# Seven products in place of eight for three pairs of cross-attention query blocks and five pairs of gate blocks

## The chip, the cores and the metric

The kernel runs on one core of one Trainium2 chip. The metric is the device time of one execution in microseconds (us). TensorE is called PE here, VectorE DVE or Vector, ScalarE ACT or Scalar, GpSimd POOL, and SyncE SP.

## The reference

Two transformer blocks are applied one after the other to one sequence of 512 tokens with 1024 features, all in float32. The two projections that the change touches are the queries of block 1's cross-attention to a memory of 256 rows, and the two kinds of gates of block 2:

```python
# block 1
x = x + hybrid_mixer(rmsnorm(x, norm_mix), ...)
h = rmsnorm(x, norm_xa)
q = (h @ w_q).reshape(b, s, 4, 256)          # xa_wq, 1024 x 1024
scores = einsum('bshd,bmhd->bhsm', q, k) * 256 ** -0.5
x = x + (softmax(scores) @ v) @ w_o          # xa_wo
x = x + squared_relu_mlp(rmsnorm(x, norm_ffn), w1, w2)
x = rmsnorm(x, norm_final)
# block 2
u = rmsnorm_2(x, norm_mix_w)
cb, cc, cx, q, k, v, g_conv, g_attn = split(u @ w_in + b_in)   # w_in_2
y_conv = (cb * causal_dwconv(cc * cx)) @ w_conv_out
y_attn = sliding_window_attention(rope(q), rope(k), v) @ w_attn_out + b_attn_out
merged = sigmoid(g_conv) * y_conv + sigmoid(g_attn) * y_attn
x = x + merged @ w_mix_out
... a gated feed-forward network with a causal convolution, and a last norm
```

Each of `g_conv` and `g_attn` is 1024 columns wide.

## The kernel before, in words

**Layout.** Everything is kept transposed: features lie on the 128 partitions, the 512 tokens along the free dimension. A projection to 128 output columns (a block, numbered n) over 1024 inputs is eight weight tiles of 128 x 128.

**Products.** PE works in the type f32r. For accuracy every operand is split into a high part, rounded to f32r, and a low part, the rest; `mm3` (L482 to L484) multiplies one weight tile with one operand in three matmuls (high by high, high by low, low by high). A plain block is 24 matmuls of 512 columns.

**Weights.** They stream from DRAM in the order in which `weight_order` lists them, eight tiles (1024 columns) in a unit. `prefetch` loads a unit into one of `NRAW` raw buffers, Scalar writes the high part (L279) and Vector the low part (L281) into one of `NWS` pairs of buffers `whi` and `wlo`. A weight index counts the tiles used. `defer(n, f)` emits f when the index has advanced by n, and `flush` does so for what is due. The order of issue on SP is that of the program. The other engines' orders are made by a list scheduler, which takes the program's order as priority and lets ready work go ahead.

**Seven products.** Twenty-six pairs of blocks (in the two feed-forward networks) are computed in the Strassen-Winograd manner. `pairg` takes two blocks and two halves of the tokens as a 2 x 2 problem, and makes seven products instead of eight, each over four pairs p of input blocks: 84 matmuls of 256 columns for two blocks. The products are ordered 1, 5, 2, 7, 3, 6, 4 (`SEVEN`, L364). `seven_steps` makes the weight sums of a pair from two raw units and splits them (L318, L326, L331, L336, L339). `rights` makes the operands on the other side: for each p, two scaled copies on Scalar (L426, L427), five operations of 256 columns on Vector (L432 to L437), and two splits (L550, L551), which leave V and W of that p in four buffers that last. Products 1, 2 and 3 use only the plain split activations; products 5 and 7 need V, 6 and 4 need W. The two results of a pair are put together in a tile `q`: after product 5 a copy of the first bank (L401), then, after the products, L407, L408, L409 and L410, which read the other three banks. The second of the two results comes out negated.

**Buffers.** `NSLOT` buffers of 2 KB (tag `t2`) hold all other tiles of 512 columns, `NQ` the tiles `q`. Eight PSUM banks are split into four `mm` and four `sm`; `bank(kind)` hands out the four of a kind in turn.

**Cross-attention.** After `w_out`, `q_g` computes the eight query blocks, n from 0 to 7, and splits them. Each of four heads needs two of them. `drive` runs the heads, which are chains of short dependent steps, and fills PE in between with `q_g` and then `wo_g` (the first part of the output projection `xa_wo`).

**Block 2's gates.** `gated_g` computes gate 30, then `w_conv_out_2` (eight blocks), then the gates 31 to 37, each a plain block, multiplied with `rb` (the row norm), put through a sigmoid and multiplied into `yc`. Between them it emits `norm_x(n)` (L1442), which scales x for the residual. After the attention, a loop computes the gates 38 to 45, each followed by a block of `w_attn_out_2` (four tiles), and splits the merged result for `w_mix_out_2`.

Of the kernel before, what the change touches and what calls it, by code (L numbers as in the profile page):

```python
# [18 lines left out]
T = 512  # L19
D = 1024  # L20

NSLOT = 67
NRAW, NWS = 4, 5

NSR, NQ = 2, 2


SPREAD = [6, 2]
# [31 lines left out]
def weight_order():  # L60


    seq = []
    seven = set()

    def pair(name, n1, n2):
        assert len(seq) % 8 == 0
        seven.add(len(seq) // 8)
        for n, o in ((n1, 0), (n2, 1), (n1, 1), (n2, 0)):
            for k in range(o, 8, 2):  # L70
                seq.append((name, k, n))

    def cols(name, ns, ks):
        for n in ns:
            for k in ks:
                seq.append((name, k, n))

    def rows(name, ks, ns):
        for k in ks:
            for n in ns:  # L80
                seq.append((name, k, n))

    r8 = range(8)
    for lo in (12, 8, 16):
        cols("w_in", range(lo, lo + 4), r8)
    rows("w_in", r8, range(4, 8))
    cols("w_in", range(0, 4), r8)
    cols("w_in", range(20, 24), r8)
    cols("xa_wk", r8, r8)
    rows("xa_wv", r8, range(4))  # L90
    rows("xa_wv", r8, range(4, 8))
    cols("w_out", range(NWO), range(4))
    cols("w_out", range(NWO), range(4, 8))
    cols("w_out", range(NWO, 8), r8)
    cols("xa_wq", r8, r8)
    cols("xa_wo", range(4), range(6))
    cols("xa_wo", range(4), (6, 7))
    cols("xa_wo", range(4, 8), r8)
    for what, i, g in ffn_order():
        if what == 1 and i < NPLAIN:  # L100
            cols("ffn_w1", (2 * i, 2 * i + 1), r8)
        elif what == 1:
            pair("ffn_w1", 2 * i, 2 * i + 1)
        else:
            cols("ffn_w2", [i], range(8 * g, 8 * g + 8))

    cols("w_in_2", [28, 29, 24, 25, 26, 27], r8)
    for i in range(8):
        cols("w_in_2", [8 + i, 16 + i, i], r8)
    cols("w_in_2", [30], r8)  # L110
    cols("w_conv_out_2", r8, r8)
    cols("w_in_2", range(31, 38), r8)
    for i in range(8):
        cols("w_in_2", [38 + i], r8)
        cols("w_attn_out_2", [i], range(4))
    cols("w_mix_out_2", r8, r8)
    for what, i, g in ffn2_order():
        if what == 2:
            cols("w_ffn_down_2", [i], range(*GROUPS2[g]))
        elif i in SEVEN2:  # L120
            pair("w_ffn_up_2", i, 22 + i)
        else:
            cols("w_ffn_up_2", [i, 22 + i], r8)
    cols("w_ffn_down_2", r8, range(*GROUPS2[2]))
    return seq, seven
# [64 lines left out]
def _build(ctx, tc, nc, A, out, stage):  # L190
# [18 lines left out]
    def tmp(shape=(P, T)):  # L209
        return ap_.tile(list(shape), F32, tag="t2", bufs=NSLOT, name=nm("tmp"))  # L210

# [29 lines left out]
    def col(name, i=0, n=1):  # L241
        o = COFF[name][0] + i
        return colt[:, o:o + n]
# [166 lines left out]
        V.tensor_tensor(q4[:, 1:3, :], b3(3), q4[:, 1:3, :], op=ALU.add)  # L410
        then(q)

    def rights(x, gname, xs):


        H = T // 2
        f = lambda hl, j: (hl[0][:, j * H:(j + 1) * H], hl[1][:, j * H:(j + 1) * H])
        res = [{} for _ in range(len(xs) // 2)]
        steps = []

        def one(p):
            st = {}

            def s0():
                st["a"], st["b"] = t2(), t2()
                S.activation(st["a"], x[2 * p], AF.Copy, scale=col(gname, 2 * p))  # L426
                S.activation(st["b"], x[2 * p + 1], AF.Copy, scale=col(gname, 2 * p + 1))  # L427

            def s1():
                a, b = st["a"], st["b"]  # L430
                st["v"], st["w"] = v, w = t2(), t2()
                V.tensor_sub(v[:, H:], b[:, H:], a[:, H:])  # L432
                V.scalar_tensor_tensor(out=w[:, :H], in0=a[:, H:], scalar=1.0, in1=a[:, :H],
                                       op0=ALU.mult, op1=ALU.subtract)
                V.tensor_scalar_mul(v[:, :H], w[:, :H], -1.0)
                V.tensor_sub(w[:, :H], w[:, :H], b[:, H:])
                V.scalar_tensor_tensor(out=w[:, H:], in0=w[:, :H], scalar=-1.0, in1=b[:, :H],  # L437
                                       op0=ALU.mult, op1=ALU.subtract)

            def s2():  # L440
                vs = split(st["v"])
                ws = split(st["w"])
                res[p].update({"B11": f(xs[2 * p], 0), "B21": f(xs[2 * p + 1], 0), "B22": f(xs[2 * p + 1], 1),
                               "V1": f(vs, 0), "V7": f(vs, 1), "V6": f(ws, 0), "T4": f(ws, 1)})

            return [s0, s1, s2]

        for p in range(len(xs) // 2):
            steps.extend(one(p))
        return res, steps  # L450
# [793 lines left out]
    os_ = []  # L1244
    qq = []

    def q_g():
        for n in range(8):
            ps = bank()
            yield from ling("xa_wq", n, range(8), xs, ps)  # L1250
            qq.append(split(ps))

    def head(h):
        while len(qq) < 2 * h + 2:
# [72 lines left out]

    rb2 = acc_tile()
    wide_later(acc, 1e-6, rb2, WIDE1, True)
    rops, steps = rights(x, "norm_ffn", xs)  # L1330
    for j, f in enumerate(steps):
        defer(1 + VD * (j // 3) + j % 3, f)
    cosT, sinT = acc_tile(), acc_tile()
# [123 lines left out]
        V.tensor_mul(t, ps, rb)  # L1457
        return t

    def biased(n):  # L1460
        g = proj_g(n)
        while True:
            try:
                next(g)
            except StopIteration as e:
                return e.value

    def rope(n, t, then):

# [166 lines left out]
            cs_.append((hi, lo))  # L1636

    yc = []

    def gated_g():  # L1640
        sg0 = None
        for n in range(-1, 8):
            if n == -1:
                t = yield from proj_g(30)
                sg0 = t2()
                S.activation(sg0, t, AF.Sigmoid, bias=col("b_in_2", 30))
                continue
            ps = bank()
            yield from ling("w_conv_out_2", n, range(8), cs_, ps)
            y = t2()  # L1650
            if n == 0:
                V.tensor_mul(y, ps, sg0)
            else:
                S.copy(y, ps)
            yc.append(y)
        for i in range(1, 8):
            norm_x(i - 1)
            t = yield from proj_g(30 + i)
            S.activation(t, t, AF.Sigmoid, bias=col("b_in_2", 30 + i))
            V.tensor_mul(yc[i], yc[i], t)  # L1660
        norm_x(7)

    bg.append(kvq_g())
    bg.append(conv2_g())
# [3 lines left out]
    flush()  # L1668
    ms = []
    for i in range(8):  # L1670
        t = biased(38 + i)
        g = tmp()
        S.activation(g, t, AF.Sigmoid, bias=col("b_in_2", 38 + i))
        ps = lin("w_attn_out_2", i, range(4), at)
        V.scalar_tensor_tensor(out=g, in0=ps, scalar=col("b_attn_out_2", i), in1=g, op0=ALU.add, op1=ALU.mult)
        V.tensor_add(yc[i], yc[i], g)
        ms.append(split(yc[i]))
# [12 lines left out]
    rb = acc_tile()  # L1690
    wide_later(acc, 1e-5, rb, 8, False)

    rops2, steps = rights(x, "norm_ffn_w_2", xs)
    for j, f in enumerate(steps):
        defer(8 + 10 * (j // 3) + 2 * (j % 3), f)

# [227 lines left out]
```

## Time and profile before

| | |
|---|---|
| median of three runs | 1541.34 us (1540.96 to 1542.74) |
| the profiled execution | 1543.6 us, of which the span of the trace is 1541.8 |
| mean granted clock of PE | 0.995 |
| PE busy | 1507.0 us of the span |
| Vector busy | 1074.0 us |
| Scalar busy | 707.1 us |
| matmuls | 8336 |

Busy times are sums over an engine's instructions. Matmuls follow each other in a pipeline, so their cost in a dense stretch is read from the distance between starts, not from their listed durations.

### The profile page before, as it was taken

How to read it: one execution, taken by the hardware profiler on the slowest of the kernel's cores; microseconds unless marked ns; L12 is line 12 of the kernel's file. 1: busy time of each engine (PE TensorE's matmuls, PEld its weight loads, DVE VectorE, ACT ScalarE, POOL GpSimd, SP SyncE). 2: the span in 40 equal slices, each digit the busy share in tenths (PEclk: the TensorE clock that was granted, in tenths of full speed). 3: DMA queues.
4: the chain of work that ended last, by engine and by line, in shares of the span. 5: the costliest groups of instructions: out<-in, count | busy, mean ns of one | idle time of the engine just before them, and what ended most of it. 6: DMA issues, size and time to landing. Idle time of an engine off the chain costs nothing.

```text
span 1541.8 us, 21393 instructions
## 1 busy us (share of the span) xinstructions
PE 1507.0 (98%) x8336; PEld 1290.3 (84%) x8336; DVE 1074.0 (70%) x1759; ACT 707.1 (46%) x1169; POOL 150.8 (10%) x162
## 2 busy tenths in 40 slices
PE   8999999999999999999999999999999998999996
PEld 6888898888888888989888888888888887898986
DVE  6897675554786786767688767335547887779757
ACT  5665555443564353535444434333334443344333
POOL 0002120200201202011400000000020001101201
PEclk9999999999999999999999999999999999999998
DMA  6033335221223223324044222222222222323311
GB/s 254 17 114 94 116 125 204 95 69 55 82 69 110 96 90 109 109 83 137 14 143 138 82 82 83 72 94 94 96 96 82 82 82 96 98 80 110 125 54 55
DMA packets 51509, 149.94 MB, mean 97 GB/s; under 512 B 9552, under 2 KB 14032, under 8 KB 51408
## 3 DMA queue, kind: packets, MB, share of 16 engines
q1 hardware_dynamic: 51264, 148.32, 28.5%
q8 instruction: 65, 1.06, 0.3%
q14 instruction: 36, 0.29, 0.1%
q10 hardware_dynamic: 144, 0.26, 0.1%
HBM read 143.97 MB, written 3.28 MB: 96 GB/s over the span
## 4 chain that ended last, share of the span: by engine, by line
PE 92%; DVE 4%; ACT 2%; issue 1%; DMA 1%; POOL 0%; SPq 0%; DVEq 0%; ACTq 0%; POOLq 0%
PE mm L482 26%; PE mm L483 25%; PE mm L484 25%; PE sm L484 3%; PE sm L482 3%; PE sm L483 3%; ACT whi L279 1%; DMA raw<-wts 1%; DVE wlo L281 0%; ACT t L1111 0%; PE sm L602 0%; DVE t L1825 0%; PE sm L920 0%; PE sm L1597 0%; PE sm L1596 0%
## 5 line engine op out<-in xcount | busy, mean ns | idle before, releaser
L482 PE MATMUL mm<-t,whi 128*128 128x512 f32 (+1 forms) x1840 | 686.0, 373 | 9.3 <-ACT whi L275 7.1
L483 PE MATMUL mm<-t,whi 128*128 128x512 f32 (+1 forms) x1840 | 682.9, 371 | 0.2 <-DVE t L551 0.2
L484 PE MATMUL mm<-t,wlo 128*128 128x512 f32 (+1 forms) x1840 | 682.5, 371 | 0.0
L482 PEld LDWEIGHTS mm<-t,whi 128*128 128x128 f32 x1840 | 347.4, 189 | 70.3 <-ACT whi L275 7.1
L484 PEld LDWEIGHTS mm<-t,wlo 128*128 128x128 f32 x1840 | 347.2, 189 | 63.3 <-DVE wlo L281 0.5
L483 PEld LDWEIGHTS mm<-t,whi 128*128 128x128 f32 x1840 | 347.4, 189 | 61.2 <-DVE t L551 0.7
L279 ACT CAST whi<-raw 128x1024 fp32r<-128x1024 f32 x202 | 211.2, 1051 | 303.6 <-PE mm L483 142.8
L281 DVE TENSOR_TENSOR wlo<-raw,whi 128x1024 fp32r<-128x1024 f32 x184 | 228.6, 1243 | 75.8 <-ACT whi L279 75.4
L596 POOL TENSOR_TENSOR acc<-acc,tmp 128x512 f32<-128x512 f32 (+1 forms) x37 | 52.7, 1430 | 467.7 <-ACT tmp L592 467.4
L482 PE MATMUL sm<-t,whi 128*128 128x256 f32 (+1 forms) x320 | 90.9, 284 | 2.9 <-ACT whi L326 2.9
L483 PE MATMUL sm<-t,whi 128*128 128x256 f32 (+1 forms) x320 | 90.8, 284 | 1.6 <-DVE t L551 1.6
L484 PE MATMUL sm<-t,wlo 128*128 128x256 f32 (+1 forms) x320 | 90.9, 284 | 0.8 <-DVE wlo L331 0.8
L331 DVE TENSOR_TENSOR wlo<-sraw,whi 128x1024 fp32r<-128x1024 f32 x52 | 68.8, 1325 | 30.9 <-ACT whi L326 30.6
L326 ACT CAST whi<-sraw 128x1024 fp32r<-128x1024 f32 x52 | 54.6, 1049 | 70.5 <-PE mm L483 59.9
L1457 DVE TENSOR_TENSOR tmp<-mm,acc 128x512 f32<-128x512 f32 x46 | 31.7, 690 | 49.0 <-PE mm L484 46.9
L482 PEld LDWEIGHTS sm<-t,whi 128*128 128x128 f32 x320 | 60.2, 188 | 4.0 <-ACT whi L326 3.3
L1414 POOL TENSOR_TENSOR res<-res,tmp 128x512 f32<-128x512 f32 x24 | 39.0, 1637 | 248.4 <-DVE tmp L1412 236.8
L483 PEld LDWEIGHTS sm<-t,whi 128*128 128x128 f32 x320 | 60.2, 188 | 2.5 <-DVE t L551 1.8
L484 PEld LDWEIGHTS sm<-t,wlo 128*128 128x128 f32 x320 | 60.4, 189 | 1.5 <-DVE wlo L331 1.0
L326 ACT CAST whi<-raw 128x1024 fp32r<-128x1024 f32 x26 | 27.3, 1050 | 51.7 <-PE mm L483 24.9
L318 DVE TENSOR_TENSOR sraw<-raw,raw 128x1024 f32<-128x1024 f32 x26 | 34.4, 1325 | 21.6 <-DMA raw<-wts 21.6
L1744 POOL TENSOR_TENSOR res<-res,tmp 128x512 f32<-128x512 f32 x16 | 27.6, 1734 | 164.9 <-DVE tmp L1743 164.9
(384 smaller groups left out, 1998.1 us busy)
## 6 DMA issues: line engine op xcount, KB each, us to landing
raw<-wts SPq DMA_DIRECT2D x259, 512.0 KB, 3.3
res<-xT SPq DMA_DIRECT2D x16, 256.0 KB, 5.2
yT<-t SPq DMA_DIRECT2D x6, 256.0 KB, 2.2
tmp<-tmp SPq DMA_DIRECT2D x20, 64.0 KB, 2.0
gm<-gm SPq DMA_DIRECT2D x4, 256.0 KB, 4.6
dn<-ch SPq DMA_DIRECT2D x4, 256.0 KB, 2.3
tmp<-memT SPq DMA_DIRECT2D x4, 256.0 KB, 2.6
cst<-const SPq DMA_DIRECT2D x1, 576.0 KB, 6.8
```

What stands on the lines that cost most here:

```text
L279: S.copy(hi, r)
L281: defer(LO, lambda r=r, hi=hi, lo=lo: V.tensor_sub(lo, r, hi.bitcast(F32)))
L318: V.tensor_tensor(t["s75"].rearrange("p (a b) -> p a b", a=2), r3, r1[:, T:].unsqueeze(1).to_broadcast([P, 2, T]), op=ALU.add)
L326: S.copy(t[n][0], s)
L331: V.tensor_sub(t[n][1], src(), t[n][0].bitcast(F32))
L482: PE.matmul(ps, lhsT=ahi, rhs=bhi, start=start, stop=False)
L483: PE.matmul(ps, lhsT=ahi, rhs=blo, start=False, stop=False)
L484: PE.matmul(ps, lhsT=alo, rhs=bhi, start=False, stop=stop)
L596: eng.tensor_add(acc[:, :w], acc[:, :w], dst[:, :w])
L1414: G.tensor_add(x[n], x[n], t)
L1457: V.tensor_mul(t, ps, rb)
L1744: G.tensor_add(x[n], x[n], t)
```

## The change

Blocks 2 to 7 of `xa_wq` become three pairs, (2,3), (4,5) and (6,7), all on `mm` banks; blocks 0 and 1 stay plain. A new set of right-hand operands is made for them by `rights`, deferred by 1 to 12 weight tiles. Of block 2's gates, 31 to 33 stay plain, and five pairs are made: (34,35) and (36,37) in `gated_g`, (38,39), (40,41) and (42,43) in the loop, each of the latter followed by two blocks of `w_attn_out_2`; 44 and 45 stay plain. Their operands are made by `rights` too, deferred by 1 to 18 tiles from the end of `w_conv_out_2`. Because `rights` reads x, the eight `norm_x` are emitted after the pair (36,37). `NSLOT` goes from 67 to 65, `NWS` from 5 to 6 and `NQ` from 2 to 1. The argument of `rights` becomes a function that gives a column, and `biased` is divided in two, without effect on the other calls.

```diff
-NSLOT = 67
-NRAW, NWS = 4, 5
+NSLOT = 65
+NRAW, NWS = 4, 6
-NSR, NQ = 2, 2
+NSR, NQ = 2, 1
...
-    cols("xa_wq", r8, r8)
+    cols("xa_wq", (0, 1), r8)
+    for n in (2, 4, 6):
+        pair("xa_wq", n, n + 1)
...
-    cols("w_in_2", range(31, 38), r8)
-    for i in range(8):
+    cols("w_in_2", (31, 32, 33), r8)
+    for i in (34, 36):
+        pair("w_in_2", i, i + 1)
+    for i in range(0, 8, 2):
+        if i < 6:
+            pair("w_in_2", 38 + i, 39 + i)
+            cols("w_attn_out_2", [i, i + 1], range(4))
+    for i in (6, 7):
         cols("w_in_2", [38 + i], r8)
         cols("w_attn_out_2", [i], range(4))
...
-    def rights(x, gname, xs):
+    def rights(x, gcol, xs):
...
-                S.activation(st["a"], x[2 * p], AF.Copy, scale=col(gname, 2 * p))
+                S.activation(st["a"], x[2 * p], AF.Copy, scale=gcol(2 * p))
...
+    ropsq, steps = rights(x, lambda n: col("norm_xa", n), xs)
+    for j, f in enumerate(steps):
+        defer(1 + 3 * (j // 3) + j % 3, f)
+
     def q_g():
-        for n in range(8):
+        for n in range(2):
             ps = bank()
             yield from ling("xa_wq", n, range(8), xs, ps)
             qq.append(split(ps))
+        for n in (2, 4, 6):
+            r = []
+            def then(q):
+                r.extend([split(q[:, :T]), split(q[:, T:], -1.0)])
+            yield from pairg("xa_wq", n, n + 1, ropsq, then, "mm")
+            qq.extend(r)
...
+    def proj2_g(n, kind):
+        r = []
+        def then(q):
+            for j in range(2):
+                t = tmp()
+                V.tensor_mul(t, q[:, j * T:(j + 1) * T], rb)
+                S.activation(t, t, AF.Sigmoid, bias=col("b_in_2", n + j), scale=1.0 - 2 * j)
+                r.append(t)
+        yield from pairg("w_in_2", n, n + 1, ropsg, then, kind)
+        return r
...
-        for i in range(1, 8):
-            norm_x(i - 1)
+        res, steps = rights(x, lambda n: gf2[:, n:n + 1], xs)
+        ropsg.extend(res)
+        for j, f in enumerate(steps):
+            defer(1 + 5 * (j // 3) + j % 3, f)
+        for i in (1, 2, 3):
             t = yield from proj_g(30 + i)
             S.activation(t, t, AF.Sigmoid, bias=col("b_in_2", 30 + i))
             V.tensor_mul(yc[i], yc[i], t)
-        norm_x(7)
+        for i in (4, 6):
+            ts = yield from proj2_g(30 + i, "mm" if i == 4 else "sm")
+            for j in range(2):
+                V.tensor_mul(yc[i + j], yc[i + j], ts[j])
+        for i in range(8):
+            norm_x(i)
...
     for i in range(8):
-        t = biased(38 + i)
-        g = tmp()
-        S.activation(g, t, AF.Sigmoid, bias=col("b_in_2", 38 + i))
+        if i < 6:
+            if i % 2 == 0:
+                gates = list(run(proj2_g(38 + i, "sm" if i % 4 else "mm")))
+            g = gates[i % 2]
+        else:
+            t = biased(38 + i)
+            g = tmp()
+            S.activation(g, t, AF.Sigmoid, bias=col("b_in_2", 38 + i))
         ps = lin("w_attn_out_2", i, range(4), at)
```

## Rows read from the trace of the kernel before

**Rows 1.** The page: busy time by engine; the chain that ended last.
```profile
PE 1507.0 (98%) x8336; PEld 1290.3 (84%) x8336; DVE 1074.0 (70%) x1759; ACT 707.1 (46%) x1169; POOL 150.8 (10%) x162
...
PE 92%; DVE 4%; ACT 2%; issue 1%; DMA 1%; POOL 0%; SPq 0%; DVEq 0%; ACTq 0%; POOLq 0%
```

**Rows 2.** Windows: stretch, busy PE, PEld, DVE, ACT, POOL, clock, DMA share, GB/s.
```profile
265.00:296.70 31.70, 31.70 (x139) 25.62 (x138) 16.50 (x20) 13.49 (x19) 9.75 (x6) 1.00 0.30 100
296.70:388.00 91.30, 91.30 (x462) 76.50 (x461) 46.73 (x90) 36.98 (x71) 0.00 (x0) 1.00 0.19 64
968.00:1010.00 42.00, 42.00 (x214) 35.35 (x213) 11.56 (x14) 13.11 (x19) 0.00 (x0) 1.00 0.26 88
1010.00:1120.00 110.00, 110.00 (x476) 89.02 (x475) 55.57 (x66) 36.92 (x45) 0.00 (x0) 1.00 0.28 94
```

**Rows 3.** Timeline of PE: start, duration, instruction; gates, then a pair.
```profile
1025.33 0.40 PE L482 MATMUL mm<-t,whi 128*128 128x512 f32 x1
...
1036.45 0.40 PE L482 MATMUL mm<-t,whi 128*128 128x512 f32 x1
...
448.12 0.28 PE L482 MATMUL sm<-t,whi 128*128 128x256 f32 x1
...
458.04 0.28 PE L482 MATMUL mm<-t,whi 128*128 128x256 f32 x1
```

**Rows 4.** Waits of PE: who on whom, us in all, times, longest.
```profile
PE mm L482 <- DVE tmp L1743: 4.0, 1, 4.0
PE sm L482 <- ACT whi L326: 2.9, 2, 1.8
...
PE sm L484 <- DVE wlo L331: 0.8, 1, 0.8
```

**Rows 5.** Groups by line: instruction, count, busy us, mean ns, idle before.
```profile
L331 DVE TENSOR_TENSOR wlo<-sraw,whi 128x1024 fp32r<-128x1024 f32 x52 | 68.8, 1325 | 30.9 <-ACT whi L326 30.6 <-PE sm L484 0.3
L318 DVE TENSOR_TENSOR sraw<-raw,raw 128x1024 f32<-128x1024 f32 x26 | 34.4, 1325 | 21.6 <-DMA raw<-wts 21.6
L281 DVE TENSOR_TENSOR wlo<-raw,whi 128x1024 fp32r<-128x1024 f32 x184 | 228.6, 1243 | 75.8 <-ACT whi L279 75.4
L407 DVE TENSOR_TENSOR q<-mm,t 128x512 f32<-128x512 f32 x13 | 8.9, 686 | 8.2 <-PE mm L484 8.2
L409 DVE TENSOR_TENSOR q<-sm,q 128x256 f32<-128x256 f32 x13 | 5.5, 420 | 0.1
L1442 DVE SCALAR_TENSOR_TENSOR res<-res,colt,acc 128x512 f32<-128x512 f32 x8 | 5.5, 746 | 0.2 <-ACT acc L612 0.2
```

**Rows 6.** Timeline of ACT and DVE at the start of the MLP.
```profile
414.23 1.23 DVE L331 TENSOR_TENSOR wlo<-raw,whi 128x1024 fp32r<-128x1024 f32 x1 [0.21 <-ACT whi L326]
415.24 0.71 ACT L426 ACTIVATE t<-res,colt 128x512 f32<-128x512 f32 x1
...
431.92 0.72 ACT L426 ACTIVATE t<-res,colt 128x512 f32<-128x512 f32 x1
...
437.65 0.68 DVE L551 TENSOR_TENSOR t<-t,t 128x512 fp32r<-128x512 f32 x1
```

**Rows 7.** Timeline of ACT and PE at the start of the cross-attention.
```profile
298.50 0.62 ACT L592 ACTIVATE tmp<-res 128x512 f32<-128x512 f32 x1
...
309.49 0.40 PE L484 MATMUL mm<-t,wlo 128*128 128x512 f32 x1
```

**Rows 8.** Timeline of DVE after the second pair of the MLP.
```profile
463.31 0.42 DVE L409 TENSOR_TENSOR q<-sm,q 128x256 f32<-128x256 f32 x1
```

**Rows 9.** Windows around a wait of PE in block 2's feed-forward network.
```profile
1279.00:1283.00 4.00, 0.05 (x1) 0.00 (x0) 3.13 (x6) 2.13 (x4) 0.00 (x0) 0.94 0.38 131
1283.00:1289.30 6.30, 6.22 (x29) 6.22 (x30) 1.13 (x2) 0.00 (x0) 2.93 (x3) 0.50 0.24 86
```

**Rows 10.** Timeline of DVE: last read of one `q`, first write of another.
```profile
1397.73 0.68 DVE L1711 SCALAR_TENSOR_TENSOR tmp<-q,tmp 128x512 f32<-128x512 f32 x1
...
1400.07 0.68 DVE L407 TENSOR_TENSOR q<-sm,t 128x512 f32<-128x512 f32 x1
```

More of the change, by code (lines that the diff above doesn't have):

```diff
@@ L425, in s0 @@
                 st["a"], st["b"] = t2(), t2()
-                S.activation(st["a"], x[2 * p], AF.Copy, scale=col(gname, 2 * p))
-                S.activation(st["b"], x[2 * p + 1], AF.Copy, scale=col(gname, 2 * p + 1))
+                S.activation(st["a"], x[2 * p], AF.Copy, scale=gcol(2 * p))
+                S.activation(st["b"], x[2 * p + 1], AF.Copy, scale=gcol(2 * p + 1))
             def s1():
@@ L1329, in _build @@
     wide_later(acc, 1e-6, rb2, WIDE1, True)
-    rops, steps = rights(x, "norm_ffn", xs)
+    rops, steps = rights(x, lambda n: col("norm_ffn", n), xs)
     for j, f in enumerate(steps):
@@ L1458, in proj_g, with run @@
         return t
-    def biased(n):
-        g = proj_g(n)
+    def run(g):
         while True:
@@ L1466, in biased @@
                 return e.value
+    def biased(n):
+        return run(proj_g(n))
     def rope(n, t, then):
@@ L1638, in _build @@
     yc = []
+    ropsg = []
+    def proj2_g(n, kind):
[8 more added lines that the diff above has]
+        return r
     def gated_g():
@@ L1691, in _build @@
     wide_later(acc, 1e-5, rb, 8, False)
-    rops2, steps = rights(x, "norm_ffn_w_2", xs)
+    rops2, steps = rights(x, lambda n: col("norm_ffn_w_2", n), xs)
     for j, f in enumerate(steps):
```

## The prediction

> **What bounds the kernel now.** I read the page first. PE is busy 98% of the span and 92% of the chain that ended last is PE; Vector, at 70%, is the next engine [rows 1]. So the time is nearly the sum of the matmuls, and a change pays if it takes matmul time away without making PE wait. Then I cut the span into the stages that the change touches [rows 2]: the last part of `w_out` ahead of the cross-attention, the cross-attention, `w_conv_out_2`, and the gates with `w_attn_out_2`. In all four PE is busy for the whole stretch. Vector is busy 16.50 of 31.70 us, 46.73 of 91.30, 11.56 of 42.00 and 55.57 of 110.00: half idle, and that idle half is what the change spends. Third, PE's timeline in one plain stretch and in one seven-product pair gives the price of each form [rows 3]. Last, the waits of PE for the whole run [rows 4] show what the 26 pairs that the kernel already has cost in stalls.
>
> **What the change removes.** Two plain column blocks are 48 matmuls of 512 columns. From the first to the 49th such start takes 1036.45 - 1025.33 = 11.12 us, 0.2317 each. A pair is 84 matmuls of 256 columns: 458.04 - 448.12 = 9.92 us, 0.1181 each [rows 3]. One pair therefore saves 1.20 us, and three and five pairs 9.6 us. Half the width is not quite half the time: 2 x 0.1181 against 0.2317 is 4.5 ns lost on each two. The Trainium skill (Perfetto Trace Analysis, Matmuls) says that larger matmuls are the more efficient ones, which speaks against this change; the rows agree and put its size at 42 x 4.5 ns = 0.19 us a pair. Without it the gain would be 11.1.
>
> **What it adds on Vector.** A pair's weights take a sum of 1024 columns (1.325 us), three low parts of 1024 (1.325 each) and three operations of 512 (0.69 each): 7.4 us, in place of two plain low parts of 1.243. The four evacuations into `q` add 3 x 0.69 + 0.42 = 2.5 [rows 5]. That is 4.9 + 2.5 = 7.4 us more per pair. One call of `rights` is, for each of four p, five operations of 256 columns and two low parts of 512: 5 x 0.42 + 2 x 0.69 = 3.5, so 14 us a call. In the cross-attention Vector goes from 46.7 to 46.7 + 3 x 7.4 + 14 = 83 us, less the first pair's weights (4.9) made earlier, so about 78 of the 91.3 - 3.6 = 87.7 us that remain. In the gates it goes from 55.6 to 55.6 + 5 x 7.4 + 14 = 107, and `norm_x`, which before was free to run early, adds 8 x 0.75 = 6: 113, for 110 - 6 = 104 us. But the first pair's weights can be made while `w_conv_out_2` runs, where Vector idles 30 of 42 us, and `norm_x` is needed only by the additions after the stage. That leaves some 100 of 104. Both stages fit, the second barely.
>
> **The other seven pairs.** The six largest waits that fall into pair work (from 4.0 down to 0.8) sum to 12.1 us over 26 pairs [rows 4], 0.47 us a pair. Seven pairs at that rate: 3.3 us. The bounds are 0, where none waits, and 8.5 us, which is all of Vector's 112.5 less 104 if nothing moves out of the gates' stage.
>
> **The first cross-attention pair.** Its product order is 1, 5, 2, 7, 3, 6, 4; products 1, 2 and 3 need only the plain operands, and product 5 needs V of all four p, which `rights` makes. Before the gates this is no matter: three plain blocks, 24 weight tiles or 24 x 3 x 0.2317 = 16.7 us, stand ahead of the pair. In the cross-attention only two blocks stand ahead. The normalised activations are complete at about 299.1 (the last square starts at 298.50), and PE ends the second block at 309.49 + 0.4 = 309.9 [rows 7]. In the MLP, where the same helper runs, the first copy starts at 415.24, the fourth p's copy at 431.92, so 5.56 us a p, and the last V is done at 437.65 + 0.68, 6.4 us behind that copy [rows 6]. At that pace V is complete here at 299.1 + 3 x 5.56 + 6.4 = 322.2. If the schedule draws forward products 2 and 3 and the half of 5 that is ready, PE has 14 of the 28 quarters, 14 x 3 x 0.1181 = 5.0 us, and works until 314.9: it would wait 7.3. In strict order it works until 312.3.
> But 5.56 is a pace under other work: at 414 Vector was making the low part of weights wanted only at 438 [rows 6]. By the operations alone a p is 3.5 us of Vector and less of Scalar. With 4.4 us a p and a tail of 4.3 (two copies 1.4, three of Vector's operations 1.3, the split 1.3 and a little latency), V is complete at 299.1 + 13.2 + 4.3 = 316.6 and the wait is 1.8. I take this, nearer the low end, because ahead of it Vector is idle 15.2 of 31.7 us [rows 2], in which the first pair's weights can be made. Head 0, which waits for the second block's split, now follows the same queue; I add 0.7 for that, an operation's length. Together 2.5 us; the bounds are 0.5 and 11.2 (7.3, 0.9 and the clock below), 2.5 more in strict order.
>
> **Three pairs in a row on the same banks.** All three take the `mm` banks, while the pairs of before alternate in the stretch I read. Product 5 of the next pair, 12 x 0.1181 = 1.42 us after its start, reuses the bank that L409 reads last. In one pair L409 ended at 463.31 + 0.42, 5.7 us after its pair's last matmul near 458.04 [rows 3, 8]: a wait of 4.3. With Vector free, the three evacuations up to it (0.69 + 0.69 + 0.42) are done before the product needs it: 0. Heads' matmuls stand between two pairs here; I take 0.25 for each of two transitions, 0.5 in all, and 0 to 8.6 as bounds.
>
> **Buffers.** A sixth weight buffer (`NWS`) lets casts run further ahead: the largest wait for casts of pair weights, 2.9 [rows 4], could halve, worth 1.5. One `q` instead of two delays L407 only if it comes before the earlier q's last read. The closest that I found is 1397.73 + 0.68 against 1400.07 [rows 10]: 1.7 us clear. For that and the two slots taken away I set 1.0 against it, and take a gain of 0.5; the bounds are a gain of 2.9 and a loss of 1.5. The DMA bytes do not change.
>
> **Sum.** 1543.6 - 9.6 + 3.3 + 2.5 + 0.5 - 0.5 = 1539.8 for the profiled execution (span 1541.8 and 1.8 outside it). The median of the three runs is 1541.34, 2.3 lower: **1537.5**, 0.25% faster.
>
> **Rivals.**
> A, the forecast: 1534.5 to 1540.
> B, nothing waits: the first pair waits under 1, the sixth buffer takes the cast waits away. 1541.3 - 9.6 + about 1.3 = 1533, 1531.5 to 1534.5. For it: Vector's idle half in all four stages. Against: every stage with pairs shows some waits.
> C, Vector becomes the bound: at 100 of 104 us in the gates, or 78 of 87.7 with latency-bound heads beside it, PE waits 3 to 7 us more than in A. 1540.5 to 1544.4, no change that can be measured (0.2%, 3.1 us, is about what a measurement of this kernel can tell). For it: the counts above. Against: Vector need not be punctual, since the next work on PE is mostly several us ahead.
> D, slower: `rights` keeps the MLP's pace in the cross-attention and PE stands 7.3 us before product 5. An idle stretch costs twice. Here, after 4.0 us in which one matmul ran, the granted clock was 0.50 (1.2 GHz) for the next 6.3 us, where 29 matmuls took 0.217 instead of 0.118 each [rows 9]: 2.9 lost. 1543.6 - 9.6 + 3.3 + 11.2 = 1548.5, or 1546 in the median's terms. It decides from about 5.3 us a p. For it: 5.56 measured in the only comparable place. Against: Vector's load there. The Trainium skill (TensorE: Matmul & The Clock Gate, HAM oscillation) says that gaps in PE's work bring the slow clock back; by that rule, which the trace agrees with at 0.50, D's wait cannot come without the extra 2.9.
> E, slower by the shared banks: L409 comes as late at both transitions between the three pairs as in the one shown, 4.3 us twice in place of 0.5. 1539.8 + 8.1 = 1547.9, 1545.6 in the median's terms. It decides from about 4 us a transition. For it: Vector is busier here. Against: heads' matmuls come between the pairs, and the four evacuations are only 2.5 us of work. The Trainium skill (Perfetto Trace Analysis, Matmuls) wants independent groups to rotate through the banks, so that the evacuation of one overlaps the next; that is this rival, and no stretch of this trace has two pairs in a row on the same banks to settle it.
> That the change does not do what it says would show in the count of matmuls.
>
> **How the numbers follow.** A 0.46 (0.36 of it below 1538.3), B 0.16, C 0.18, D 0.16, E 0.04. Faster by over 0.2% is below 1538.3: 0.36 + 0.16 = 0.52. Slower is above 1544.4: D and E, 0.20. Within: 0.10 + 0.18 = 0.28. The range reaches from B's low end to where A, B, C and the mildest of D are in: 1531.5 to 1545. A's own range is 1534.5 to 1540.
>
> **What would show it.** PE's matmul count should be 8336 + 8 x 36 = 8624. In the cross-attention, product 5 of the first pair should wait about 2 us on a low part of V, with the clock at 1.00; over 4 us and a clock of 0.50 behind it is D. Between its pairs, a wait of PE released by L409 would show the shared banks. In the gates, the stage should be some 4 us shorter than 110, with Vector near 95%; waits of PE on Vector's low parts over 3 us there are C. Waits for casts should be fewer per pair than 26 pairs had. The prediction is wrong if the heads, held by late queries, leave PE without filler at the stage's end, where I assume enough `xa_wo` work.

## The result, and the profile after

The changed kernel takes 1553.28 us (median of 4 runs, 1551.36 to 1556.7) against 1542.04 us before (4 runs): ratio 1.0072, 95% interval 1.0059 to 1.0085. It is slower by 11 us, on the other side of the forecast and outside its range. The profiled execution took 1555.03 us, its span is 1553.2.

Busy times by engine and the chain that ended last, from the page of the kernel after:

```profile
PE 1507.9 (97%) x8624; PEld 1302.3 (84%) x8624; DVE 1144.4 (74%) x1887; ACT 740.5 (48%) x1225; POOL 151.0 (10%) x162
...
PE 89%; DVE 6%; ACT 2%; issue 1%; DMA 0%; POOL 0%; DVEq 0%; SPq 0%; ACTq 0%
```

Against [rows 1] there are 288 matmuls more, 8 x 36, as the change says. But PE is busy as long as before instead of 9.6 us less, and PE's share of the chain fell from 92% to 89%, while Vector's rose from 4% to 6%. The first is for the most part slow clock: where the granted clock is 0.50 (1.2 GHz), a matmul of 256 columns is listed with about 0.41 us, elsewhere with 0.28. The second is waits.

To see where, I cut both spans at instructions that both kernels have: the last addition after `w_out`, the last after `xa_wo`, the norm after the MLP, the last copy of `w_conv_out_2`, the first addition after `w_mix_out_2`, and the end. The marks come from the view by source line. Line numbers after are 8 to 50 higher than before. For the last mark but one, the kernel before:

```profile
L1682 DVE TENSOR_TENSOR res<-res,mm x8: 686/689/690, 1120.9 to 1159.8; 128x512 f32<-128x512 f32 x8
```

The same view of the kernel after (count, shortest, median and longest in ns, first and last start):

```profile
L1732 DVE TENSOR_TENSOR res<-res,mm x8: 686/689/690, 1134.3 to 1173.3; 128x512 f32<-128x512 f32 x8
```

The addition that began at 1120.9 now begins at 1134.3, 13.4 us later. All stages, in us of the profiled executions:

| stage | before | after | difference | what the matmuls alone would give |
|---|---|---|---|---|
| to the end of `w_out` | 297.1 | 295.8 | -1.3 | 0 |
| cross-attention | 116.2 | 120.0 | +3.8 | -3.6 |
| MLP | 350.9 | 351.8 | +0.9 | 0 |
| block 2 to the end of `w_conv_out_2` | 246.1 | 247.0 | +0.9 | 0 |
| gates and `w_attn_out_2` | 110.6 | 119.7 | +9.1 | -6.0 |
| the rest | 420.9 | 418.9 | -2.0 | 0 |

So 7.4 us are lost in the cross-attention and 15.1 in the gates; outside the two changed stages 1.5 us are gained. The two stages as windows, the gates first, then the cross-attention (columns as in [rows 2]), and four short windows in the gates:

```profile
1014.60:1134.30 119.70, 110.13 (x658) 98.47 (x657) 97.17 (x143) 55.17 (x77) 0.00 (x0) 0.94 0.28 93
295.80:415.80 120.00, 115.96 (x678) 101.23 (x677) 89.74 (x160) 64.18 (x115) 10.15 (x6) 0.99 0.24 80
...
1035.00:1038.50 3.50, 0.49 (x5) 0.28 (x3) 3.50 (x7) 2.94 (x5) 0.00 (x0) 0.91 0.00 0
1038.50:1043.00 4.50, 3.95 (x15) 3.36 (x16) 4.33 (x11) 1.31 (x4) 0.00 (x0) 0.50 0.37 118
...
1092.00:1098.40 6.40, 0.47 (x4) 0.26 (x3) 6.23 (x10) 3.94 (x7) 0.00 (x0) 0.80 0.72 237
1098.40:1103.00 4.60, 4.52 (x21) 4.37 (x22) 0.89 (x2) 0.30 (x2) 0.00 (x0) 0.53 0.33 114
```

PE stands still twice in the gates, and behind each stop its clock is at half speed, as in [rows 9]. Vector is busy 97.17 of 119.70 us, and nearly all of both stops. The waits of PE in the whole run, largest first (columns as in [rows 4]):

```profile
PE mm L490 <- ACT t L334: 8.7, 2, 6.0
PE mm L490 <- ACT whi L283: 6.9, 1, 6.9
PE mm L492 <- DVE t L339: 3.4, 4, 1.3
PE mm L490 <- DVE res L1462: 3.1, 1, 3.1
PE sm L492 <- DVE wlo L339: 2.1, 3, 0.9
```

The second stood before too, with 7.1 at the very start of the kernel. Of the first, 2.7 us lie in the MLP, where the same wait was 1.5 before; the 6.0 us are new. `L334` writing a `t` is the high part of the weight block that product 2 uses, the only one of a pair's weights that lies in the slots of tag `t2`. The fourth names `norm_x` (L1462), but `norm_x` is nothing that a matmul reads. A releaser is inferred; PE's next matmul, at 1038.56, is product 2 again, of the pair (34,35), and the split that it reads was cast on Scalar just before:

```profile
1037.91 0.60 ACT L334 CAST t<-raw 128x512 fp32r<-128x512 f32 x1
...
1038.56 0.58 PE L490 MATMUL mm<-t,t 128*128 128x256 f32 x1 [3.07 <-DVE res L1462]
```

Around the larger wait (timeline of PE, Vector and Scalar):

```profile
1092.19 0.28 PE L492 MATMUL mm<-t,wlo 128*128 128x256 f32 x1
...
1094.65 1.40 DVE L1725 SCALAR_TENSOR_TENSOR tmp<-mm,colt,tmp 128x512 f32<-128x512 f32 x2
1095.97 1.29 DVE L1726 TENSOR_TENSOR t<-t,tmp 128x512 f32<-128x512 f32 x2
...
1096.74 1.16 ACT L558 CAST t<-t 128x512 fp32r<-128x512 f32 x2 [2.03 <-DVE t L1726]
1097.81 0.61 ACT L334 CAST t<-raw 128x512 fp32r<-128x512 f32 x1
...
1098.48 0.58 PE L490 MATMUL mm<-t,t 128*128 128x256 f32 x1 [6.01 <-ACT t L334]
1098.86 0.42 PE L491 MATMUL mm<-t,t 128*128 128x256 f32 x1
```

What PE can do of the pair (42,43) without product 2's weights ends at 1092.19. Product 2's split is cast at 1097.81, right after Scalar split the merged results 2 and 3 (L558), which had waited for Vector's additions (L1726), which stood in Vector's queue. Its raw weights needed nothing of that. In program order the split does come after: `w_attn_out_2` leaves only eight tiles between the pairs (40,41) and (42,43), and the six preparation steps are emitted two tiles apart, so the last two, with product 2's split, are emitted only where the pair starts, behind the splits of the merged results. The pair (40,41), with the same eight tiles, did not wait: PE had 23 matmuls of the next two blocks of `w_attn_out_2` to run, from 1076.77 on, before its product 2 at 1082.11. The first theory, then: a small tile that depends on nothing late takes its slots behind tiles that wait for Vector.

In the cross-attention (timeline of Scalar, then PE):

```profile
298.00 0.71 ACT L434 ACTIVATE t<-res,colt 128x512 f32<-128x512 f32 x1
...
303.58 0.72 ACT L434 ACTIVATE t<-res,colt 128x512 f32<-128x512 f32 x1
...
309.47 0.72 ACT L434 ACTIVATE t<-res,colt 128x512 f32<-128x512 f32 x1
...
310.71 0.56 ACT L558 CAST t<-mm 128x512 fp32r<-128x512 f32 x1
311.17 0.62 ACT L334 CAST t<-raw 128x512 fp32r<-128x512 f32 x1
...
316.32 0.72 ACT L434 ACTIVATE t<-res,colt 128x512 f32<-128x512 f32 x1
...
311.32 0.38 PE L490 MATMUL sm<-t,t 128*128 128x256 f32 x1 [1.00 <-ACT t L558]
...
312.89 0.50 PE L492 MATMUL sm<-t,t 128*128 128x256 f32 x2 [0.83 <-DVE t L559]
...
314.48 0.58 PE L492 MATMUL mm<-t,t 128*128 128x256 f32 x1 [0.87 <-DVE t L339]
...
319.53 0.38 PE L490 MATMUL mm<-t,whi 128*128 128x256 f32 x1 [0.78 <-ACT t L558]
320.35 0.39 PE L491 MATMUL mm<-t,whi 128*128 128x256 f32 x1 [0.43 <-DVE t L559]
```

The first copies of the four p start 5.6, 5.9 and 6.9 us apart, the MLP's pace or slower [rows 6]. Behind the copies of the third p stand the split of query block 0 (L558 on `mm`, at 310.71; in the kernel before L550 did it at 304.44) and product 2's split (L334, at 311.17). PE's waits here sum to only 3.9 us, in five short ones: 1.00 and 0.83 for block 0's split, which head 0 reads, 0.87 for product 2's split, and 0.78 and 0.43 for V. Between them run a few matmuls of head 0 and of product 2, and the clock halves for a while all the same: from 311 to 321, 36 matmuls run in 10 us, which at 0.118 each would take 4.2.

### The profile page after: what moved, and what is told of

Read it like the earlier page. It is cut to its first block, busy times and chain, and to the rows that moved or that the text cites. A ratio compares the mean times of both kernels' runs of the same rounds, so it can differ in the third digit from the quotient of the medians.

```text
span 1553.2 us, 22216 instructions
## 1 busy us (share of the span) xinstructions
PE 1507.9 (97%) x8624; PEld 1302.3 (84%) x8624; DVE 1144.4 (74%) x1887; ACT 740.5 (48%) x1225; POOL 151.0 (10%) x162
## 4 chain that ended last, share of the span: by engine, by line
PE 89%; DVE 6%; ACT 2%; issue 1%; DMA 0%; POOL 0%; DVEq 0%; SPq 0%; ACTq 0%
PE mm L490 24%; PE mm L492 24%; PE mm L491 24%; PE sm L492 4%; PE sm L490 4%; PE sm L491 4%; DVE wlo L289 1%; DVE wlo L339 1%; DVE t L559 0%; ACT whi L287 0%; DVE t L339 0%; ACT t L1119 0%; ACT whi L334 0%; DVE tmp L1630 0%; DMA res<-xT 0%
## 5 line engine op out<-in xcount | busy, mean ns | idle before, releaser
L490 PE MATMUL mm<-t,whi 128*128 128x512 f32 (+1 forms) x1856 | 677.1, 365 | 8.5 <-ACT whi L283 6.9
L491 PE MATMUL mm<-t,whi 128*128 128x512 f32 (+1 forms) x1856 | 673.3, 363 | 1.0 <-DVE t L559 1.0
L492 PE MATMUL mm<-t,wlo 128*128 128x512 f32 (+1 forms) x1856 | 673.0, 363 | 0.1
L289 DVE TENSOR_TENSOR wlo<-raw,whi 128x1024 fp32r<-128x1024 f32 x164 | 204.5, 1247 | 38.2 <-ACT whi L287 37.6
L334 ACT CAST whi<-sraw 128x1024 fp32r<-128x1024 f32 x68 | 71.3, 1050 | 108.1 <-PE mm L491 88.2
L339 DVE TENSOR_TENSOR wlo<-sraw,whi 128x1024 fp32r<-128x1024 f32 x68 | 88.1, 1295 | 34.8 <-ACT whi L334 34.7
L492 PE MATMUL sm<-t,wlo 128*128 128x256 f32 (+1 forms) x368 | 104.6, 284 | 2.1 <-DVE wlo L339 2.1
L491 PE MATMUL sm<-t,whi 128*128 128x256 f32 (+1 forms) x368 | 104.2, 283 | 0.7 <-DVE t L559 0.7
L490 PE MATMUL sm<-t,whi 128*128 128x256 f32 (+1 forms) x368 | 104.2, 283 | 0.3 <-ACT whi L334 0.3
L491 PEld LDWEIGHTS sm<-t,whi 128*128 128x128 f32 x368 | 69.3, 188 | 1.6 <-DVE t L559 0.9
L490 PEld LDWEIGHTS sm<-t,whi 128*128 128x128 f32 x368 | 69.3, 188 | 1.2 <-ACT whi L334 0.5
L1434 POOL TENSOR_TENSOR res<-res,tmp 128x512 f32<-128x512 f32 x24 | 39.2, 1650 | 249.5 <-DVE tmp L1432 240.3
L334 ACT CAST whi<-raw 128x1024 fp32r<-128x1024 f32 x34 | 35.7, 1051 | 56.9 <-PE mm L491 33.4
L490 PE MATMUL mm<-t,t 128*128 128x256 f32 x156 | 46.6, 299 | 11.8 <-ACT t L334 8.7
L339 DVE TENSOR_TENSOR wlo<-raw,whi 128x1024 fp32r<-128x1024 f32 x34 | 43.1, 1266 | 12.7 <-ACT whi L334 12.6
```

The costliest lines, as they stand in the source:

```text
L289: defer(LO, lambda r=r, hi=hi, lo=lo: V.tensor_sub(lo, r, hi.bitcast(F32)))
L334: S.copy(t[n][0], s)
L339: V.tensor_sub(t[n][1], src(), t[n][0].bitcast(F32))
L490: PE.matmul(ps, lhsT=ahi, rhs=bhi, start=start, stop=False)
L491: PE.matmul(ps, lhsT=ahi, rhs=blo, start=False, stop=False)
L492: PE.matmul(ps, lhsT=alo, rhs=bhi, start=False, stop=stop)
```

## The experiments

All ratios are to runs of the kernel before on the same chip. "Stage" means the marks above.

**1. The counts alone.** The kernel before with `NSLOT` 65, `NWS` 6, `NQ` 1.

```diff
-NSLOT = 67
-NRAW, NWS = 4, 5
+NSLOT = 65
+NRAW, NWS = 4, 6
-NSR, NQ = 2, 2
+NSR, NQ = 2, 1
```


> The kernel before with only the changed counts (65 slots, 6 weight buffers, 1 q). Theory 1 (the loss lies in late operands at the start of pairs): the marks outside the two changed stages moved by -1.3, +0.9, +0.9 and -2.1 us, so about -1.6 us in all, 1540 us. Rival (the single q and the two slots taken away are what costs): 3 us or more slower than before.


1543.32 us, ratio 1.0002 (0.9993 to 1.0010): no difference, so the counts are not the loss. Inside, the rest of block 2 is 1.9 us shorter (the wait of 4.0 us [rows 4] is gone), and the MLP 1.3 longer: its first pair waits 2.7 us for product 2's split, before 1.5, because the split stands behind the second hidden tile, and that now waits for the one `q`.

**2 and 3. Each half alone.** Queries in pairs with plain gates, and the reverse.

> The changed kernel with the gates left plain (three query pairs, new counts). Theory 1: the cross-attention took 3.8 us more between the marks, with -1.6 from the counts about +2.2 us against before, 1544 us. Rival (the queries' pairs gain their 3.6 us and only the gates lose): 1536 to 1538 us.


1546.56 us, 1.0021 (1.0013 to 1.0030).

> The changed kernel with the queries left plain (five gate pairs, new counts). Theory 1: the gates took 9.1 us more between the marks, with -1.6 about +7.5 us, 1549.5 us. Rival (the two stages disturb each other, or the loss is the queries'): less than +4 us.


1552.7 us, 1.0064 (1.0052 to 1.0076). The stages take 119.9 and 118.9 us, nearly what they take together (120.0 and 119.7): the two losses are separate, and both times came out some 3 us above what was expected, of which 1.6 is what the counts were taken to give and did not.

**4. Product 2's split first.** For the eight new pairs, in `seven_steps`:

```diff
+        if order[u * 8][0] in ("xa_wq", "w_in_2"):
+            return op, [
+                both(hi("b", b), s75, hi("a", a)),
+                both(lo("b", b), lo("a", a), hi("s75s", c)),
+                both(s6, s4),
+                both(lo("s75s", c), hi("s64s", d)),
+                lo("s64s", d),
+                end,
+            ]
```


> The changed kernel; for the eight new pairs the split of the weight block that product 2 uses stands first among a pair's six preparation steps instead of fifth and sixth. Theory 1 (that split comes late because its two slots are handed out in program order, behind tiles that wait for Vector): the waits of 6.0 and 3.1 us in the gates go, with the 2 to 3 us of slow clock behind each; 8 to 11 us less than the changed kernel, 1542 to 1545 us. Rival 2 (Vector's amount of work bounds the gates): the waits move to another operand and the time stays within 2 us of 1553.


1544.17 us, 1.0014 (1.0004 to 1.0024): 9 us less than the changed kernel with the same work on every engine. The gates take 110.3 us. The wait of 6.0 is gone, the one of 3.1 became 2.1. The cross-attention hardly moved (119.5). With 65 slots as before, the split comes early where it is emitted early. What is left of the wait of 3.1 has another cause (timeline of Vector and PE in this run):

```profile
1035.68 0.68 DVE L1486 TENSOR_TENSOR tmp<-mm,acc 128x512 f32<-128x512 f32 x1
...
1036.41 0.39 PE L499 MATMUL mm<-t,t 128*128 128x256 f32 x1 [2.12 <-DVE tmp L1486]
```

L1486 empties the `mm` bank of a plain gate, and product 2 of the pair (34,35), on `mm` banks too, starts 0.05 us after its end. In the changed kernel the same instruction (L1477) ended at 1037.25, 1.3 us before the split: two late items, of which the split came last.

**5. The same place in the program, other buffers.** The split goes into a pair of `whi` and `wlo` instead of two `t2` slots.

```diff
-                t[n] = (wd(F32R, "whi", NWS), wd(F32R, "wlo", NWS)) if w > T else (t2(F32R), t2(F32R))
+                t[n] = (wd(F32R, "whi", NWS), wd(F32R, "wlo", NWS)) if w > T or order[u * 8][0] in ("xa_wq", "w_in_2") else (t2(F32R), t2(F32R))
+                t[n] = tuple(a[:, :w] for a in t[n])
```


> The changed kernel; for the eight new pairs the split of product 2's weight block goes into a pair of the whi and wlo buffers instead of two of the 65 slots, at the same place of the program. Theory 1a (the slots are handed out in program order, so the split waits behind tiles that wait for Vector): the split comes early and the 6.0 us wait goes, 1543 to 1547 us. Theory 1b (Scalar's instruction order alone puts it there): it stays behind, 1551 to 1555 us.


1544.5 us, 1.0016 (1.0006 to 1.0025), again some 9 us less than the changed kernel. Scalar's timeline of this run, around the same pair:

```profile
1075.51 1.22 ACT L559 CAST t<-t 128x512 fp32r<-128x512 f32 x2 [0.29 <-DVE t L1727]
1081.26 0.62 ACT L335 CAST whi<-raw 128x512 fp32r<-128x512 f32 x1
1089.04 0.62 ACT L559 CAST t<-t 128x512 fp32r<-128x512 f32 x1 [1.46 <-DVE t L1727]
```

The split (L335) is now cast 7.8 us ahead of the splits of the merged results (L559 at 1089.04) that it stood behind before. It was emitted at the same place; only the tag of its buffers differs. So Scalar's order by the program does not hold it, the buffers of its tag do. Experiments 4 and 5 fit slots of one tag that are handed out in program order, so that a tile whose inputs are ready does not overtake one whose inputs are not. The profile shows no slots, though, and this edit also leaves two of the 65 free for each pair: that all were taken just then is not ruled out, since no run gives the changed kernel more of them. The gates take 107.2 us. The cross-attention got worse (121.3): product 5 there waits 2.5 us.

**6. The operands overlapped.** In both new calls of `rights` the steps of p+1 start before those of p are done.

```diff
-        defer(1 + 3 * (j // 3) + j % 3, f)
+        defer(1 + j // 3 + 2 * (j % 3), f)
...
-            defer(1 + 5 * (j // 3) + j % 3, f)
+            defer(1 + j // 3 + 2 * (j % 3), f)
```


> The changed kernel; the three steps of rights for the four p overlap (steps of p+1 start before those of p are done) in both new calls, instead of one p after the other. Theory 1 (the 5.6 us a p are the length of a chain of dependent steps run one p after the other): under 4.5 us a p, V complete 3 us or more earlier in the cross-attention, 3 to 6 us less than the changed kernel, 1547 to 1550 us. Rival 2 (Vector's amount of work sets the pace): V as late as before, within 2 us of 1553.


1550.11 us, 1.0053 (1.0040 to 1.0067), 3.2 us less than the changed kernel. The 5.6 us a p are a chain of dependent steps, and not an amount of work: now the first copies of the four p start within 5.4 us (298.32 to 303.69), and in the cross-attention V is complete at about 315.5 instead of 320.3. In the gates the wait of 3.1 us is gone and the stage takes 113.9; in the cross-attention it did not help (120.7): with two plain blocks ahead PE still waits 1.2 and 2.4 us for low parts of V, and from 314 to 320 the granted clock is 0.50.

**7. Both.** Product 2's split first, and the operands overlapped.

> Product 2's split first, and the steps of rights overlapped. Theory 1: both effects add, 1538 to 1541 us, at or below the kernel before. Rival 2: no better than the split first alone, 1544 us.


1548.77 us, 1.0037 (1.0025 to 1.0050): the effects do not add, and it is 4.6 us above experiment 4 (3.5 by the ratios; the two ran on different chips). The gates take 110.0, no less than with the split first alone; a new wait of 3.1 us stands there, for L1734, the evacuation of a block of `w_attn_out_2`. The cross-attention takes 120.0. The rest of the difference to experiment 4 lies outside the two changed stages, 0.8 to 1.6 us in each of the others, and stays unexplained; the profiled execution of 4, from which its stages are read, took 1541.68 us, near the low end of its runs (1541.03 to 1549.22).

**8. Four plain query blocks.** As 7, but blocks 0 to 3 plain and two pairs.

```diff
-    cols("xa_wq", (0, 1), r8)
-    for n in (2, 4, 6):
+    cols("xa_wq", (0, 1, 2, 3), r8)
+    for n in (4, 6):
```


> As the one before, but four query blocks plain and two pairs, so that the operands have 22 us instead of 11 us of PE work ahead of their first use. Theory 1 (only the lead of the first pair is short): no wait there, the two pairs give their 2.4 us, 1536 to 1539 us. Rival (the heads, held by late queries, set the cross-attention's end): no less than the three pairs.


1539.67 us, 0.9985 (0.9977 to 0.9994). The cross-attention takes 114.3 us, 1.9 less than before, with no wait over 0.25 us: two pairs with time ahead of them gain, three without lose. The gates still have the wait for L1734 (timeline of Scalar, Vector and PE):

```profile
1083.10 0.60 ACT L334 CAST t<-raw 128x512 fp32r<-128x512 f32 x1
1083.13 0.75 DVE L1734 SCALAR_TENSOR_TENSOR tmp<-mm,colt,tmp 128x512 f32<-128x512 f32 x1
...
1084.03 0.55 PE L499 MATMUL mm<-t,t 128*128 128x256 f32 x1 [3.08 <-DVE tmp L1734]
```

The bank is free at 1083.88; product 2's split, though emitted first, is done only at 1083.70, hardly earlier.

**9. The last loop's gates on `sm` banks.** L1734 reads an `mm` bank, and cannot run until the pair's gates are put together; the next pair on `mm` banks needs that bank for product 2.

```diff
-                gates = list(run(proj2_g(38 + i, "sm" if i % 4 else "mm")))
+                gates = list(run(proj2_g(38 + i, "sm")))
```


> As the run with four plain query blocks, but all three gate pairs of the last loop on sm banks, so that no product needs a bank that still holds a block of w_attn_out_2. Theory 1: the last wait in the gates (3.1 us on L1734) and the slow clock behind it go, 4 to 6 us less: 1534 to 1536 us. Rival (a pair after a pair on the same banks waits for L409's successor instead, as in rival E of the prediction): 1538 us or more.


1534.73 us, 0.9947 (0.9934 to 0.9959): 0.5% faster than before. The gates take 105.5 us. Product 2's split now comes early too:

```profile
1077.94 0.61 ACT L334 CAST t<-raw 128x512 fp32r<-128x512 f32 x1
```

So the edit took both late items away, and does not tell the bank from the split. The expected rival shows as one wait of 0.7 us at 1046.81, for the copy of the first `sm` bank after product 5 (L418). What PE still waits for (waits, largest first) is the start of the kernel and, below it, what the feed-forward pairs waited for before, there 1.5 and 0.8:

```profile
PE mm L499 <- ACT whi L283: 6.8, 1, 6.8
PE mm L499 <- ACT t L334: 2.7, 1, 2.7
PE sm L501 <- DVE wlo L339: 2.2, 3, 1.0
```

**10. The mended gates alone,** with all query blocks plain.

> The gates of the run above (split first, operands overlapped, sm banks) with all eight query blocks plain. Theory 1 (five pairs are worth 6.0 us once nothing waits): 1536 to 1538 us. Rival 2 (Vector's amount of work in the gates keeps part of it): 1539 us or more.


1536.06 us, 0.9957 (0.9944 to 0.9971). The gates in one window:

```profile
1010.20:1115.80 105.60, 104.91 (x658) 94.18 (x657) 96.22 (x143) 54.66 (x77) 0.00 (x0) 1.00 0.33 105
```

Vector is busy 96.22 of 105.60 us, 91%, and PE 104.91: Vector's amount of work does not hold PE. With 110.6 before, the five pairs give 5.0 of the 6.0 us.

**11. Four plain query blocks alone,** without the other edits.

> The changed kernel with four plain query blocks and two pairs, nothing else. Theory 1 (the queries lose by a lead that is 11 us short, at 5.6 us a p): the wait in the cross-attention goes and the loss of 3.8 us there becomes a gain of about 2; 5 to 6 us less than the changed kernel, 1547 to 1549 us. Rival (the lead is not the cause): within 2 us of 1553.


1554.57 us, 1.0075 (1.0062 to 1.0089): a miss. The cross-attention takes 119.5 us as with three pairs. Timeline of this run, Scalar and PE:

```profile
315.71 0.72 ACT L434 ACTIVATE t<-res,colt 128x512 f32<-128x512 f32 x1
...
321.11 0.58 ACT L558 CAST t<-mm 128x512 fp32r<-128x512 f32 x1
321.74 0.39 PE L490 MATMUL sm<-t,t 128*128 128x256 f32 x1 [0.49 <-ACT t L558]
...
329.13 0.63 ACT L334 CAST t<-raw 128x512 fp32r<-128x512 f32 x1
...
331.16 0.39 PE L492 MATMUL mm<-t,t 128*128 128x256 f32 x1 [0.84 <-DVE t L339]
```

The operands were in time and product 5 did not wait. But the split of query block 1 (L558 on `mm`, at 321.11), finished by PE at about 310, came only after the copies of the last p (315.71): a plain block's split takes slots as well, behind the operands. Head 0 and the banks wait for it, and product 2's split (329.13) stands behind further ones. Lead alone was the wrong theory; it takes lead and a short chain.

**12. The mended kernel with the old counts.** Experiment 9 with 67 slots, 5 weight buffers and 2 `q`.

> The run with the gates on sm, with the counts of before (67 slots, 5 weight buffers, 2 q). Theory 1: counts are worth little as in the run of the counts alone, within 2 us of the run with the new ones. Rival (the pairs need the sixth weight buffer): 3 us or more above it.


1537.88 us, 0.9970 (0.9958 to 0.9981), 3.2 us above experiment 9: the rival's bound by the time, but not by the place. The cross-attention takes 114.2 us against 114.4 and the gates 106.8 against 105.5; most of the difference lies at both ends (to `w_out` 297.6 against 295.7, the rest 420.2 against 417.4), where the change touches nothing but the counts. Waits for casts of pair weights are back (1.8), one of 1.7 on the copy after product 5, and one of 3.0 in the last stage, which was 4.0 before. Why the counts alone gave nothing (1) and give 3 us here is not shown.

**13 and 14. Which tile was late in the cross-attention.** Experiment 9 with one edit taken back for the query pairs: the overlap of the operands (13), the split first (14).

```diff
     ropsq, steps = rights(x, lambda n: col("norm_xa", n), xs)
     for j, f in enumerate(steps):
-        defer(1 + j // 3 + 2 * (j % 3), f)
+        defer(1 + 3 * (j // 3) + j % 3, f)
```


> The fastest kernel so far (gates on sm: split first, operands overlapped, four plain query blocks), with the query pairs' operands made one p after the other again. Theory 1 (the plain blocks' own splits take their slots behind the last p, so heads and banks wait until it is begun): the cross-attention grows by 2 to 4 us from 114.4, 1537 to 1539 us. Rival (with four plain blocks only product 2's split was late): 114 to 115 us and 1535.


1537.63 us, 0.9967 (0.9954 to 0.9980); the stage grows from 114.4 to 116.6, and the waits of 0.5 and 0.7 us for head 0's operands are back.

```diff
-        if order[u * 8][0] in ("xa_wq", "w_in_2"):
+        if order[u * 8][0] == "w_in_2":
```


> The fastest kernel so far, with product 2's split of the query pairs back at its old place (the gates keep it first). Theory 1 (it stands behind the splits of the plain blocks and of the pair before): the cross-attention grows by 2 to 4 us from 114.4, 1537 to 1539 us. Rival (only the pace of the operands matters there): 114 to 115 us and 1535.


1534.01 us, 0.9942 (0.9925 to 0.9958), with the cross-attention and the gates as windows:

```profile
296.60:410.60 114.00, 114.00 (x641) 98.62 (x640) 84.65 (x153) 61.51 (x112) 10.47 (x6) 1.00 0.23 74
1009.70:1115.30 105.60, 104.91 (x658) 94.14 (x657) 96.20 (x143) 54.66 (x77) 0.00 (x0) 1.00 0.34 105
```

The stage stays at 114.0 with PE busy all the time: here the rival was right, the split need not come first. What the query pairs need is four plain blocks ahead and the operands overlapped. This is the fastest kernel measured, together with experiment 9, and beats both the kernel before and the changed one.

## Why the prediction was wrong, point by point

**The saving was right.** The matmul count and the price of a pair held. With the stops gone the gates shrank by 5.0 us (experiment 10; 6.0 worked out) and the cross-attention by 2.2 for two pairs (experiment 14; 2.4 worked out).

**The step that failed is the term for the other seven pairs:** 3.3 us from the rate of the 26 pairs before, 0.47 each. It measured 15.1 us in the gates alone. The rate was taken from pairs that follow another pair directly or have 16 tiles or more ahead of them, where the preparation is emitted early. In the gates' last loop a pair has eight tiles ahead of it, and the split for product 2 was emitted behind tiles that wait for Vector: the 6.0 us of the pair (42,43). In the pair (34,35) it stood behind the operands: the 3.1 us. The bound of 8.5 came from Vector's amount of work, which was not the limit (experiment 10). The two waits and the half-speed matmuls behind them, about 30 and 20 at 0.21 instead of 0.118 us, 2.8 and 1.9 us, make 13.8 of the 15.1. In the terms of the sum the profiled execution lost 15.1 + 7.4 - 1.5 = 21.0 us where 3.3 + 2.5 + 0.5 - 0.5 = 5.8 was forecast; that is the whole 15.2 between 1539.8 and 1555.0.

**`norm_x` did not move out of the gates,** as the count for Vector had it. All eight ran between 1015.83 and 1041.10, three of them (2.2 us) in the first stop of PE, ahead of the low part of product 2's split. No run moves them, so what they cost is not shown.

**"Before the gates this is no matter" failed too.** The prediction set the 16.7 us of plain blocks against nothing: by its own numbers for the queries V takes 3 x 4.4 + 4.3 = 17.5 us, at the MLP's pace 23.1. The four p of the gates started at 1015.04, 1020.68, 1026.91 and 1035.39, spread over 20 us where three times the MLP's pace is 16.7. Vector had the plain gates, `norm_x` and a pair's weights to do between the steps, and product 2's split of that pair, which the prediction does not look at, stood behind the last of them.

**The first query pair was mis-sized by its pace.** I took 4.4 us a p because the operations sum to 3.5. Experiments 6 and 13 show that the pace is the length of the chain, one p after the other; it was 6.1 on average, above rival D's 5.3. V was complete at about 320.3, not 316.6. The cross-attention lost 7.4 us in place of 2.5. Its waits fell otherwise than forecast: 1.2 us for V in place of 1.8, 1.8 for head 0 in place of 0.7, and 0.9 for product 2's split, which the sum did not have. The slow pace reached PE mostly through the splits that stand behind the copies, and less through V. That is D's pace without D's one wait of 7.3; the clock at half speed came, as D had it. The Trainium skill (TensorE: Matmul & The Clock Gate, HAM oscillation) ties that clock to gaps in PE's work; the trace agrees, with granted clocks of 0.50 and 0.53 behind stops of 3.1 and 6.0 us.

**The shared banks of the query pairs cost nothing:** no wait of PE in the profile after is released by L417, as L409 is numbered now, against 0.5 taken and rival E's 8.1. Banks did hold PE elsewhere: that of a plain gate (experiment 4) and that of a block of `w_attn_out_2` (experiments 7 and 8), which the prediction does not list.

**Rival C, Vector as the bound, is out:** at 91% busy PE ran nearly without a stop (experiment 10). What Vector's load does is make each item of its queue later, and that reaches PE only through what is ordered behind it.

**The buffers were about right** with a gain of 0.5 and bounds of a gain of 2.9 and a loss of 1.5: nothing alone, 3.2 in the mended kernel, a little over the bound. The Trainium skill (Perfetto Trace Analysis, Optimization Strategy) says that recurring gaps can mean too few buffers for the next tile; the gaps here were single ones, and experiments 4 and 5 closed them with no slot added. By that rule one would have raised `NSLOT`; no run does so on the changed kernel, and experiment 12, which has two slots more but also one weight buffer less and one `q` more, is slower.

**Open.** Why experiment 7 is slower than 4, mostly outside the changed stages. Whether more slots would have done in the gates what the order did, and how much of the last wait there was the bank's. Three query pairs with a chain short enough were not found; whether starting the operands before the last addition of `w_out` would do it was not tried.

## What to carry to other kernels

When a form of work that runs well in one stage is moved to another, its rate of waits doesn't come with it: list for each operand of the first products what is emitted ahead of it under the same buffer tag and on the same engine, and what those tiles wait for, and for each bank what still has to empty it. A tile that depends on nothing late should be emitted before tiles that do, or have buffers of its own tag. Price a chain of dependent steps by its length measured elsewhere, and not by the sum of its operations; and price a stop of PE with the slow clock behind it.

## What the runs showed of the hardware that was not expected

Three waits in a row, none over 1.0 us, were followed by half the clock as the one stop of 6.0 us was. PE waited 1.00, 0.83 and 0.87 us before the matmuls at 311.32, 312.89 and 314.48, with four matmuls between each two. From 314.3 to 317.4 the granted clock is 0.50, and the matmuls from 314.86 to 317.43 start 0.21 us apart, where they take 0.118 elsewhere.
